# Q, K and V projections in two pairs of tiles, another pretended time for the first U gathers, and an output projection in plain f32

## The chip, the core and the metric

The kernel runs on one core of one Trainium2 chip. The metric is the device time of one execution in microseconds (us); the median of three runs is given. Five engines work side by side, each through its own instructions in a fixed order: TensorE (PE, with its weight loads as PEld), VectorE (DVE), ScalarE (ACT), GpSimd (POOL) and SyncE (SP). SP issues the plain DMAs, POOL the indirect ones (gathers).

## What is computed

512 tokens of 1024 features pass through two layers, all in float32. Layer 0 mixes tokens by sliding-window attention, layer 1 by a short gated convolution, and each is followed by PEER, a retrieval of experts:

```python
def peer_ffn(xn, w_query, sub_keys, expert_u, expert_v):
    q = (xt @ w_query).reshape(T, PEER_HEADS, 2, QUERY_HALF)
    s = jnp.einsum('thpd,hpnd->thpn', q, sub_keys)
    ...
    u = jnp.take(expert_u, ic, axis=0)
    a = jnp.einsum('td,thkd->thk', xc, u)
    w = gc * jax.nn.gelu(a, approximate=False)
    v = jnp.take(expert_v, ic, axis=0)
    return jnp.einsum('thk,thkd->td', w, v)

for i in range(DEPTH):
    h = rmsnorm(x, norm_mix[i])
    x = x + (attention(h) if i % 2 == 0 else short_gated_conv(h))
    h = rmsnorm(x, norm_ffn[i])
    x = x + peer_ffn(h, ...)
```

Each token picks 16 of 16384 experts for each of 8 heads, so 128 rows of `expert_u` and 128 of `expert_v`, of 4 KB each. The attention projects every token to 16 query heads, 4 key heads and 4 value heads (`w_qkv`), and its result with `w_o`.

## The kernel before

The tokens lie in four tiles of 128. PEER is done in two ways. For **tiles 2 and 3** it is dense (`dense`, L688): all 128 blocks of 128 experts are read and multiplied, and a table G of gates, zero for experts that are not picked, masks the result. One step of that loop is `ustep` (L700), three groups of eight `psA` matmuls, and `vstep` (L710), twelve `y` matmuls (L731). A float32 factor is split there into two float32r halves, high and low (`halves`, L693, one ACT cast and one DVE subtraction), and three products are summed. For **tiles 0 and 1** the picked rows are gathered (`gather`, L620): 128 U gathers (L631, 128 rows, one for each token, 512 KB), each followed by one DVE product and sum (L634), and then 128 V gathers (L662, the 128 rows of one token), of which PE takes two at a time (L672, four `acc` matmuls for a pair). Both kinds fill the same ring of six buffers (`gtile`, L612), two more in layer 1's front.

Four gathers run in the course of the kernel: layer 0 tile 0, layer 0 tile 1, layer 1 tile 0, layer 1 tile 1. They are called U0/V0, U1/V1, U2/V2 and U3/V3 here. The rest of the work is in four stages: the first front (attention, and routing of layer 0), the dense part of layer 0, the second front (convolution, routing of layer 1), and the dense part of layer 1.

The work is written as three Python generators (`stream_d` for fronts and dense parts, `stream_g` for the gathers, `stream_f` for what tiles 0 and 1 need besides), and `merge` (L810) decides in which order their pieces are written down. Each piece yields a number, the time that it is taken to last, and the stream that is furthest behind goes next. For one gather that number is `rate()` (L802): GR0 ahead of the front, the pair FR0 (U, V) in the first front, DR0 in the dense part. The order written is a priority: a scheduler then orders every engine's instructions when the kernel is built, and takes an earlier-written one first where both could go. The V matmuls get a head start (L668, HPF in the fronts and HPV in the dense parts). `stream_d` stops at `yield "g0_1"` (L921) until the gather of tile 1 in layer 0 is written: the convolution of tiles 1 to 3 begins with `xd[1]`, tile 1's result.

In the first front, `attn_qkv` (L229) projects tile 0 alone with pieces of `w_qkv` in the pool `wp` (`piece`, PE line L237); attention and routing of tile 0 follow (its first indices release U0); then it projects tiles 1, 2 and 3 with pieces in the attention's pool (`scpiece`). `attn` (L245) normalizes and rotates, makes scores, softmax and weighted values, and ends in `proj` (L181), the product with `w_o`. For tiles 1 to 3 that product is split (L189 to L200); for tile 0 it is plain f32 (L202).

Of the kernel before, what the change touches and what calls it, by code (L numbers as in the profile page):

```python
# [8 lines left out]
F32 = mybir.dt.float32  # L9
F32R = mybir.dt.float32r  # L10
# [5 lines left out]
ALU = mybir.AluOpType  # L16
# [3 lines left out]
P = 128  # L20
# [22 lines left out]
SCB = 4  # L43
# [5 lines left out]
GSC = 32768.0  # L49
GY = 1.7  # L50
FD0 = 100.0
QP = 3.0
GR0 = 1.3
DEC = 2
FD1 = 80.0
# [15 lines left out]
P3 = 1  # L71
# [3 lines left out]

DR0 = (2.4, 2.4)
DR1 = (2.5, 2.5)
FR0 = (3.0, 3.0)
FR1 = (3.0, 3.0)


# [1 line left out]
def trunk(ctx: ExitStack, tc: tile.TileContext, a: dict, out: bass.AP):  # L83
    nc = tc.nc
# [130 lines left out]
    def attn_norm(tiles, pool):  # L215
        gain = first.pop("gain", None) or gain_of(a["norm_mix"][0:1, :])
        res = []
        for t in tiles:
            if "x" in first:
                xs[t] = first.pop("x")  # L220
            else:
                xs[t] = b4.tile([P, D], F32, name="xq", tag="b4")
                nc.sync.dma_start(xs[t], a["x"][t * P:(t + 1) * P, :])
            hT = pool.tile([P, KC, P], F32, name="hTa", tag="hTa", bufs=4)
            normT(t, gain, hT, py)
            res.append(hT)
        return res
# [17 lines left out]
    def attn(tiles, qks, pool, L):  # L245
# [1 line left out]
        kT, vs, qkg, sink, nsink, cos, sin, mask = L  # L247
        nh = NH + NKV
        oTs = []
        sp = P3 and n > 1  # L250
        for j, t in enumerate(tiles):
            qk = qks[j]
            sq = pool.tile([P, nh, HD], F32, name="qsq", tag="qsq")
# [25 lines left out]
            for half in range(2):  # L279
# [3 lines left out]
                    nc.tensor.transpose(ps[:, k * P:(k + 1) * P],  # L283
                                        qk[:, 2 * hp:2 * hp + 2, :].rearrange("p a d -> p (a d)"), ident)
                nc.scalar.copy(qT[:, half * 4:half * 4 + 4, :], ps.rearrange("p (k t) -> p k t", k=4))
            if sp:
                oT = pool.tile([P, 2, 4, P], F32R, name="oTh", tag="hTa", bufs=4)
                oL = pool.tile([P, 2, 4, P], F32R, name="oTl", tag="qk", bufs=3)
            else:
                oT = oL = pool.tile([P, 2, 4, P], F32, name="oT", tag="hTa", bufs=4)  # L290
            oTs.append([(lambda k, o=o: o[:, k // 4, k % 4, :]) for o in (oT, oL)])
            if t == 0:
                k0, kw, moff, blks = 0, P, P, [0]
            else:
# [2 lines left out]
            for gp2 in range(2):  # L297
# [42 lines left out]
                    yield 6.0  # L340
                psov = pso.rearrange("p (r q) -> p r q", r=4)
                nc.scalar.copy(oT[:, gp2], psov)
                if sp:
                    nc.vector.tensor_tensor(oL[:, gp2], psov, oT[:, gp2], op=ALU.subtract)
        for t in tiles:
            xs[t] = pool.tile([P, D], F32, name="x", tag="x", bufs=3)
            nc.sync.dma_start(xs[t], a["x"][t * P:(t + 1) * P, :])
        yield from proj(a["wo"], oTs, tiles, py, (pool, ("sc", "sc"), SCB) if sp else None)

    def conv(tiles, pool, psum, slow=1.0):  # L350
        n = len(tiles)
# [506 lines left out]
    def stream_d():  # L858
        with tc.tile_pool(name="l0", bufs=1) as l0:
            def lc(name, shape, src=None):  # L860
                t = l0.tile(shape, F32, name=name)
                nc.sync.dma_start(t, a[name] if src is None else src)
                return t
            cos, sin = lc("cos", [P, NT, RH]), lc("sin", [P, NT, RH])
            mask = lc("mask", [P, 2 * P])
            qg1 = lc("qg1", [P, HD], bcast_row(a["q_norm"]))
            kg1 = lc("kg1", [P, HD], bcast_row(a["k_norm"]))
            sink = lc("sink", [P, NH], bcast_row(a["sinks"]))
            qkg = l0.tile([P, NH + NKV, HD], F32, name="qkg")
            nc.vector.tensor_copy(qkg[:, :NH, :], qg1.unsqueeze(1).to_broadcast([P, NH, HD]))  # L870
            nc.vector.tensor_copy(qkg[:, NH:, :], kg1.unsqueeze(1).to_broadcast([P, NKV, HD]))
            kT = l0.tile([P, NKV, S], F32, name="kT", tag="k8")
            vs = l0.tile([P, NT, NKV * HD], F32, name="vs")
            nsink = l0.tile([P, NH], F32, name="nsink")
            nc.vector.tensor_scalar(nsink, sink, -1.0, None, op0=ALU.mult)
            L = (kT, vs, qkg, sink, nsink, cos, sin, mask)
            flip = [0]

            def p2(name):
                flip[0] ^= 1  # L880
                return pmm(name) if flip[0] else pv.tile([P, 512], F32, name=name, tag="acc")

            def scpiece(src):
                w = l0.tile([P, KC, P], F32, name="wsc", tag="sc", bufs=SCB)
                nc.sync.dma_start(w, src)
                return w

            def run(g):
                for v in g:
                    if isinstance(v, list):  # L890
                        return v
                    yield v
            hTs = attn_norm([0], l0)
            yield 5.0
            qk0 = yield from run(attn_qkv([0], hTs, l0, L, py, piece, 1.75))
            hTs = attn_norm([1, 2, 3], l0)
            yield from attn([0], qk0, l0, L)
            r = st["p0_0"] = []
            yield from router(0, [0], None, py, None, r)
            st["r0_0"] = 1  # L900
            st["front"] = True
            st["pace"] = FS1
            qks = yield from run(attn_qkv([1, 2, 3], hTs, l0, L, p2, scpiece, QP))
            yield from attn([1, 2, 3], qks, l0, L)
            if GX0:
                st["gx"] = (l0, "sc", SCB)
            xnT = l0.tile([P, KC, 2 * P], F32, name="xnT", tag="k8")
            r = []
            yield from router(0, [1, 2, 3], l0, py, xnT, r)
# [78 lines left out]
```

## Time and profile before

| what | value |
|---|---|
| median of three runs | 3003.43 us (2999.48 to 3004.02) |
| the profiled execution | 2992.02 us, of which the span 2990.3 us |
| PE busy | 2626.9 us, 88% of the span |
| DVE busy | 2235.7 us, 75% |
| ACT busy | 1559.1 us, 52% |
| POOL busy | 1365.3 us, 46% |
| moved by DMA | 931.38 MB, mean 311 GB/s |

The span runs from the first to the last instruction of the program; the profiled execution's own time is 1.7 us longer. A share of 88% is a mean over stages: a stage in which PE is full sets its own length, one in which it is half empty has another limit. So the profile is read stage by stage below: with tables of busy time by stretch, where a count such as (x85) is the number of instructions in it; with the chain of waits that ended last; and with the instructions in order of time. In the trace an f32 matmul has two records.

### The profile page before, as it was taken

What the parts mean: (1) busy time and instruction counts of PE and PEld (TensorE: products, weight loads), DVE (VectorE), ACT (ScalarE), POOL (GpSimd) and SP (SyncE); (2) the same over time, 40 slices, a digit from 0 to 9 for tenths busy, and PEclk for the clock granted to TensorE, in tenths of its full rate; (3) what the DMA queues carried; (4) which work ended last, traced back from release to release, by engine and by line L of the source; (5) the groups of instructions that cost most, each with busy time, mean ns of one, the idle gap of its engine ahead of it and who ended that gap; (6) DMA issues with size and microseconds to landing.
All of it is one profiled execution on the core that took longest, in us unless ns stands there. A gap on an engine that the chain in (4) does not pass through costs nothing. (4 is left out here: it accounts for less than half of the span.)

```text
span 2990.3 us, 53463 instructions
## 1 busy us (share of the span) xinstructions
PE 2626.9 (88%) x19980; PEld 2083.9 (70%) x19980; DVE 2235.7 (75%) x5234; ACT 1559.1 (52%) x2384; POOL 1365.3 (46%) x1154
## 2 busy tenths in 40 slices
PE   5974699869999889999998689997888699999998
PEld 5762368636988767777787686773677577777897
DVE  2499849888998987446699774899899957446554
ACT  4224533685673458348444333358466449547543
POOL 0157733366344455534467424236566755554000
PEclk8986799989999999999999799997999899999999
DMA  5888988989999988998999867789999998998554
GB/s 199 283 315 306 341 293 276 329 308 382 365 353 389 323 318 290 345 328 291 363 408 396 310 220 279 249 319 318 363 349 360 345 359 297 333 317 302 192 189 157
DMA packets 263204, 931.38 MB, mean 311 GB/s; under 512 B 29984, under 2 KB 38560, under 8 KB 262944
## 3 DMA queue, kind: packets, MB, share of 16 engines
q0 software_dynamic: 147456, 536.94, 49.5%
q1 hardware_dynamic: 115488, 391.03, 36.3%
q8 instruction: 157, 2.57, 0.3%
q14 instruction: 103, 0.84, 0.1%
HBM read 916.31 MB, written 11.53 MB: 310 GB/s over the span
## 5 line engine op out<-in xcount | busy, mean ns | idle before, releaser
L631 POOL DMA_INDIRECT ug<-in_u_dram,idx x512 | 668.3, 1305 | 638.1 <-DVE act L634 312.5
L662 POOL DMA_INDIRECT vg<-in_v_dram,idxT x512 | 572.2, 1118 | 689.1 <-PE acc L672 571.7
L634 DVE CUSTOM_DVE_ANT_0 ug<-ug,xn 128x1024 f32<-128x1024 f32 x512 | 622.8, 1226 | 40.3 <-DMA ug<-in_u_dram,idx 39.3
L176 PE MATMUL psA<-xh,uh 128*128 128x256 f32 x2048 | 521.1, 292 | 46.0 <-ACT uh L696 19.0
L177 PE MATMUL psA<-xl,uh 128*128 128x256 f32 x2048 | 504.2, 284 | 0.0
L176 PEld LDWEIGHTS psA<-xh,uh 128*128 128x128 f32 x2048 | 391.1, 191 | 127.9 <-ACT wh L719 32.7
L697 DVE TENSOR_TENSOR ul<-du,uh 128x1024 fp32r<-128x1024 f32 x256 | 316.6, 1237 | 181.0 <-ACT uh L696 179.1
L697 DVE TENSOR_TENSOR vl<-dv,vh 128x1024 fp32r<-128x1024 f32 x256 | 316.2, 1235 | 145.2 <-ACT vh L696 121.8
L177 PEld LDWEIGHTS psA<-xl,uh 128*128 128x128 f32 x2048 | 392.0, 191 | 4.5 <-issue 0.5
L696 ACT CAST uh<-du 128x1024 fp32r<-128x1024 f32 x256 | 268.6, 1049 | 205.3 <-PE psA L177 172.6
L696 ACT CAST vh<-dv 128x1024 fp32r<-128x1024 f32 x256 | 268.5, 1050 | 162.7 <-PE y L731 139.7
L672 PE MATMUL acc<-vg,wd 128*32 128x512 f32 x2048 | 318.1, 635 | 31.4 <-DMA vg<-in_v_dram,idxT 30.9
L731 PE MATMUL y<-vh,wh 128*128 128x512 f32 x1024 | 290.2, 406 | 34.9 <-ACT vh L696 29.9
L179 PE MATMUL psA<-xh,ul 128*128 128x256 f32 x2048 | 288.7, 283 | 10.1 <-DVE ul L697 10.0
L731 PE MATMUL y<-vl,wh 128*128 128x512 f32 x1024 | 285.7, 401 | 12.8 <-DVE vl L697 12.8
L731 PE MATMUL y<-vh,wl 128*128 128x512 f32 x1024 | 285.5, 399 | 3.0 <-DVE wl L720 3.0
L179 PEld LDWEIGHTS psA<-xh,ul 128*128 128x128 f32 x2048 | 261.8, 189 | 21.8 <-DVE ul L697 16.6
L738 ACT COPY jr<-ijg 128x2048 f16<-128x2048 f16 x128 | 243.2, 1900 | 35.0 <-DVE oj L742 33.1
L731 PEld LDWEIGHTS y<-vh,wh 128*128 128x128 f32 x1024 | 179.4, 191 | 86.5 <-ACT vh L696 36.7
L731 PEld LDWEIGHTS y<-vl,wh 128*128 128x128 f32 x1024 | 190.1, 191 | 62.9 <-DVE vl L697 18.8
L731 PEld LDWEIGHTS y<-vh,wl 128*128 128x128 f32 x1024 | 194.8, 192 | 50.9 <-DVE wl L720 4.7
L742 DVE TENSOR_TENSOR oj<-jr,io 128x2048 f16<-128x2048 f16 x128 | 157.4, 1229 | 78.0 <-PE psG L751 66.7
(208 smaller groups left out, 4021.1 us busy)
## 6 DMA issues: line engine op xcount, KB each, us to landing
du<-in_uT_dram SPq DMA_DIRECT2D x256, 512.0 KB, 6.6
dv<-in_v_dram SPq DMA_DIRECT2D x256, 512.0 KB, 5.9
wpc<-in_wq_dram SPq DMA_DIRECT2D x64, 512.0 KB, 4.8
wpc<-in_w_in_dram SPq DMA_DIRECT2D x48, 512.0 KB, 5.9
wpo<-in_wo_dram SPq DMA_DIRECT2D x16, 512.0 KB, 7.5
ug<-in_u_dram,idx POOLq DMA_INDIRECT x512
vg<-in_v_dram,idxT POOLq DMA_INDIRECT x512
wpo<-in_w_out_dram SPq DMA_DIRECT2D x16, 512.0 KB, 5.2
```

The costliest lines, as they stand in the source:

```text
L176: nc.tensor.matmul(ps, w[0][:, k, :], x[0][:, k, ts], start=(k == 0), stop=False)
L177: nc.tensor.matmul(ps, w[0][:, k, :], x[1][:, k, ts], start=False, stop=False)
L179: nc.tensor.matmul(ps, w[1][:, k, :], x[0][:, k, ts], start=False, stop=(k == KC - 1))
L631: nc.gpsimd.indirect_dma_start(out=ug, out_offset=None, in_=a[f"u{l}"], in_offset=bass.IndirectOffsetOnAxis(ap=r["idx"][h][:, c:c + 1], ax ...
L634: nc.vector.tensor_tensor_reduce(out=ug, in0=ug, in1=xn, scale=1.0, scalar=0.0, op0=ALU.mult, op1=ALU.add, accum_out=act[:, s:s + 1])
L662: ld = nc.gpsimd.indirect_dma_start(out=vg, out_offset=None, in_=a[f"v{l}"], in_offset=bass.IndirectOffsetOnAxis(ap=idxT[:, tt:tt + 1], ax ...
L672: mm = nc.tensor.matmul(acc[c:c + 32, :], wd[:, j, r8, :], vgs[j][:, h * 512:(h + 1) * 512], start=(q == 0 and r8 == 0), stop=(q == 3 and ...
L696: nc.scalar.copy(hi, w)
L697: nc.vector.tensor_tensor(lo, w, hi, op=ALU.subtract)
L731: nc.tensor.matmul(ys[tt][h], x[:, tt * P:(tt + 1) * P], m[:, h * 512:(h + 1) * 512], start=first and k == 0, stop=last and k == len(terms ...
L738: nc.scalar.copy(jr, ijg[:, 0, t0:t0 + TG].unsqueeze(2).to_broadcast([P, TG, P]))
L742: nc.vector.tensor_tensor(oj, jr, io128.unsqueeze(1).to_broadcast([P, TG, P]), op=ALU.is_equal)
```

## The change

Four things are changed. `attn_qkv` is called for tiles 0 and 1 together, so each of the twelve weight pieces that it loads serves two tiles, and later for tiles 2 and 3; `attn` still runs for tile 0 first and then for 1, 2 and 3. The pretended time of the second projection's pieces goes from 3.0 to 2.0 (QP). The pretended time of a U gather in the first front goes from 3.0 to 6.0 (FR0). The output projection of tiles 1 to 3 is done in plain f32, without the halves `oTh`, `oTl`, `woh` and `wol`.

```diff
-QP = 3.0
+QP = 2.0
...
-FR0 = (3.0, 3.0)
+FR0 = (6.0, 3.0)
...
-        sp = P3 and n > 1
...
-            if sp:
-                oT = pool.tile([P, 2, 4, P], F32R, name="oTh", tag="hTa", bufs=4)
-                oL = pool.tile([P, 2, 4, P], F32R, name="oTl", tag="qk", bufs=3)
-            else:
-                oT = oL = pool.tile([P, 2, 4, P], F32, name="oT", tag="hTa", bufs=4)
-            oTs.append([(lambda k, o=o: o[:, k // 4, k % 4, :]) for o in (oT, oL)])
+            oT = pool.tile([P, 2, 4, P], F32, name="oT", tag="hTa", bufs=4)
+            oTs.append([lambda k, o=oT: o[:, k // 4, k % 4, :]])
...
-                if sp:
-                    nc.vector.tensor_tensor(oL[:, gp2], psov, oT[:, gp2], op=ALU.subtract)
...
-        yield from proj(a["wo"], oTs, tiles, py, (pool, ("sc", "sc"), SCB) if sp else None)
+        yield from proj(a["wo"], oTs, tiles, py, None)
...
-            hTs = attn_norm([0], l0)
+            hTs = attn_norm([0, 1], l0)
             yield 5.0
-            qk0 = yield from run(attn_qkv([0], hTs, l0, L, py, piece, 1.75))
-            hTs = attn_norm([1, 2, 3], l0)
-            yield from attn([0], qk0, l0, L)
+            qk01 = yield from run(attn_qkv([0, 1], hTs, l0, L, py, piece, 3.5))
+            hTs = attn_norm([2, 3], l0)
+            yield from attn([0], qk01[:1], l0, L)
...
-            qks = yield from run(attn_qkv([1, 2, 3], hTs, l0, L, p2, scpiece, QP))
-            yield from attn([1, 2, 3], qks, l0, L)
+            qks = yield from run(attn_qkv([2, 3], hTs, l0, L, p2, scpiece, QP))
+            yield from attn([1, 2, 3], qk01[1:] + qks, l0, L)
```

The changed file is seven lines shorter from L287 on, so a line number there is up to seven less (L672 is now L665).

PE at the start of the program, before (`hTa` are the normalized and transposed tokens, `psq` the projection, `psk` and `psqT` the start of tile 0's attention):

```order
L153 MATMUL psT<-ident,h 128x128 x8
L237 MATMUL psq<-wpc,hTa 128x128 x96
L153 MATMUL psT<-ident,h 128x128 x24
L276 MATMUL psk<-ident,kd 128x128 x4
L283 MATMUL psqT<-ident,qk 128x128 x8
```

and now:

```order
L153 MATMUL psT<-ident,h 128x128 x16
L237 MATMUL psq<-wpc,hTa 128x128 x192
L153 MATMUL psT<-ident,h 128x128 x16
L275 MATMUL psk<-ident,kd 128x128 x4
L282 MATMUL psqT<-ident,qk 128x128 x8
```

Tile 1's transposes and its 96 projection matmuls now stand ahead of tile 0's attention.

PE at the end of layer 0's dense part, before (`y` are the last sums of the dense part, `psT` the transposes with which the convolution of tiles 1 to 3 begins, tile 1 first, `psbcu` its matmuls):

```order
L731 MATMUL y_4419<-vl,wh 128x512
L731 MATMUL y_4420<-vl,wh 128x512
L375 MATMUL psT<-ident,h 128x128 x24
L176 MATMUL psbcu_17265<-hh,whi 128x384
L176 MATMUL psbcu_17303<-hh,whi 128x384
```

and now:

```order
L724 MATMUL y_4091<-vl,wh 128x512
L724 MATMUL y_4092<-vl,wh 128x512
L665 MATMUL acc<-vg,wd 32x512 x88
L368 MATMUL psT<-ident,h 128x128 x24
L176 MATMUL psbcu_17101<-hh,whi 128x384
```

88 `acc` matmuls, those of the last 22 pairs of V1, stand between the dense part and the convolution. Before, the last pair of V1 stood ahead of step 96 of the 128 dense steps; now the first 42 pairs stand ahead of step 88 and none between there and the end.

POOL at the same place, now (`vg` are V1's gathers and then V2's, `ug` U2's, `wd` the weights that a V gather's rows are multiplied with, `dw` products of dense steps):

```order
L655 DMA vg<-in_v_dram,idxT 128x1024 x4
L706 TENSOR_TENSOR dw<-dw,G 128x256 x13
L655 DMA vg<-in_v_dram,idxT 128x1024 x14
L647 MEMSET wd 128x512
L655 DMA vg<-in_v_dram,idxT 128x1024 x16
L655 DMA vg<-in_v_dram,idxT 128x1024 x8
L624 DMA ug<-in_u_dram,idx 128x1024 x8
L624 DMA ug<-in_u_dram,idx 128x1024 x120
L655 DMA vg<-in_v_dram,idxT 128x1024 x22
```

All 128 gathers of U2 stand behind the last of V1, in one piece with no dense product between them. In the order of before, 83 reductions of U2 stood on DVE ahead of the last `vl` of layer 0's dense part.

## Rows read from the trace of the kernel before

**Rows 1.** The page: gather queue (packets, MB, share of 16 engines), one plain load (us to landing).

```profile
q0 software_dynamic: 147456, 536.94, 49.5%
...
dv<-in_v_dram SPq DMA_DIRECT2D x256, 512.0 KB, 5.9
```

**Rows 2.** Busy time by stretch: length, PE, PEld, DVE, ACT, POOL, PEclk, DMA share, GB/s.

```profile
0.00:40.00 40.00, 27.81 (x208) 27.20 (x208) 4.30 (x11) 9.80 (x23) 1.19 (x6) 0.96 0.86 312
...
150.00:357.00 207.00, 117.09 (x683) 83.49 (x681) 201.22 (x586) 88.23 (x243) 137.88 (x116) 0.74 0.90 317
...
1453.00:1645.00 192.00, 172.65 (x1049) 147.97 (x1047) 185.91 (x284) 80.84 (x121) 128.17 (x93) 1.00 1.01 399
1645.00:1675.00 30.00, 6.24 (x26) 5.21 (x26) 27.89 (x51) 10.12 (x18) 20.47 (x17) 0.57 1.00 385
1675.00:1791.00 116.00, 104.99 (x578) 102.83 (x577) 83.53 (x138) 37.89 (x50) 33.99 (x29) 0.96 0.70 240
1791.00:1850.00 59.00, 53.13 (x262) 32.49 (x264) 22.11 (x30) 18.75 (x27) 24.82 (x22) 0.97 0.72 259
1850.00:1975.00 125.00, 123.58 (x956) 97.57 (x949) 103.34 (x542) 47.91 (x109) 42.07 (x44) 1.00 0.76 262
1975.00:2092.00 117.00, 92.14 (x1075) 58.74 (x1073) 109.61 (x434) 96.33 (x109) 64.49 (x59) 0.85 0.93 332
```

**Rows 3.** Stretches as before, instructions on the tile ug alone: DVE, POOL, PEclk, DMA, GB/s.

```profile
1453.00:1645.00 192.00, 103.11 (x85) 125.83 (x90) 1.00 1.01 399
1645.00:1675.00 30.00, 17.10 (x16) 15.85 (x13) 0.57 1.00 385
1675.00:1791.00 116.00, 35.23 (x29) 31.43 (x26) 0.96 0.70 240
```

**Rows 4.** Stretches as before, instructions on the tile acc alone: PE, PEld, ACT, the rest alike.

```profile
1453.00:1645.00 192.00, 2.99 (x24) 0.57 (x24) 2.31 (x4) 1.00 1.01 399
...
1791.00:1850.00 59.00, 15.20 (x92) 2.71 (x96) 0.00 (x0) 0.97 0.72 259
1850.00:1975.00 125.00, 29.66 (x160) 5.06 (x152) 0.00 (x0) 1.00 0.76 262
1975.00:2092.00 117.00, 37.10 (x224) 5.36 (x224) 2.31 (x4) 0.85 0.93 332
```

**Rows 5.** The ends of both dense parts, instructions on the tile y alone: PE, PEld, DVE.

```profile
1453.00:1645.00 192.00, 96.94 (x401) 72.65 (x399) 0.00 (x0) 1.00 1.01 399
...
2805.00:2978.00 173.00, 100.74 (x420) 76.82 (x420) 0.34 (x1) 1.00 0.54 176
```

**Rows 6.** Timeline of PE between two dense steps: start, us, engine, line, what, records.

```profile
1447.15 1.06 PE L672 MATMUL acc<-vg,wd 128*32 128x512 f32 x8
1448.14 0.39 PE L176 MATMUL psA<-xh,uh 128*128 128x256 f32 x1
```

**Rows 7.** Timelines of the first front: projection, output projection plain and split, DVE's splits.

```profile
23.13 16.16 PE L237 MATMUL psq<-wpc,hTa 128*128 128x128 f32 x128 [3.30 <-DMA wpc<-in_wqkv_dram]
...
43.43 1.47 DVE L259 TENSOR_TENSOR qk<-qk,qr 128x1280 f32<-128x1280 f32 x1
...
90.19 5.32 PE L202 MATMUL pswo<-wpo,oT 128*128 128x512 f32 x12
...
357.39 1.22 DVE L192 TENSOR_TENSOR wol<-wpo,woh 128x1024 fp32r<-128x1024 f32 x1
...
359.67 0.69 DVE L344 TENSOR_TENSOR oTl<-pso,oTh 128x512 fp32r<-128x512 f32 x1
...
362.00 0.39 PE L200 MATMUL pswo<-woh,oTl 128*128 128x512 f32 x1
362.23 0.40 PE L199 MATMUL pswo<-wol,oTh 128*128 128x512 f32 x1
```

**Rows 8.** Timeline at the start of the second front, ACT and POOL.

```profile
1655.26 1.06 ACT L143 ACTIVATE h<-x 128x1024 f32<-128x1024 f32 x1 [8.62 <-DMA x<-xd]
...
1656.30 0.94 POOL L631 DMA_INDIRECT ug<-in_u_dram,idx  x1 [0.31 <-issue]
```

## The prediction

> **What bounds the kernel now.** I read first the busy time by stretch. No engine sets the whole span. From 150 to 357 us, in the first front, DVE is busy 201 of 207 us and PE 117: the reductions of U0 and the attention of three tiles share DVE. In the last 192 us of layer 0's dense part PE is busy 173, DVE 186, and the DMA engines are full at 399 GB/s, since U2's gathers run beside the steps; no V work is left there but three pairs [rows 2 to 4]. Then comes a hole: for 30 us PE is busy 6.2, until tiles 1 to 3 are normalized and transposed; the convolution follows with PE busy 105 of 116 us, and the routing with 124 of 125 [rows 2]. The last stretch, 2805 to 2978 us, has no gather in it, and PE is never idle [rows 5].
>
> The gathers are a chain of their own, U0, V0, U1 to V3. It has slack at the end of the kernel (the last stretch runs without it), but one deadline: V1 must be done before the convolution begins. Before, it was done 32 steps early. What the profile must answer is what happens when that deadline is missed, since the new order of PE puts 22 of V1's 64 pairs between the last dense step and the convolution.
>
> **Why the pace does this.** FR0 relieves the first front of nothing: in the new order all 128 reductions of U0 still stand on DVE ahead of the routing of tiles 1 to 3, because DVE takes what is ready. But as a written order, every later gather moves back: at the end of layer 0's dense part by 127 places, 44 of V1 and 83 of U2. V1's tail is then written behind the dense steps, and PE, always ready with a step, takes it last. The ring holds six buffers, so POOL is three pairs ahead and then stands still.
>
> **The change, part by part.**
>
> *First front, +18 us.* 96 matmuls more (192 records) stand ahead of tile 0's attention; 128 records took 16.2 us, so 24 us [rows 7]. Some of this could lie in time that PE spends idle (12 of the first 40 us [rows 2]), but the order makes the first projection wait for tile 1's transposes too, so I count all. The twelve weight loads are the same number in all. From there DVE sets the pace, and it loses work: tile 1's three passes like that of 1.47 us and a dozen short ones (some 7 us) now lie earlier, six `oTl` of 0.69 us and three `wol` of 1.22 us are gone, two sums of some 0.7 us come in: 13 us less, and U0 ends 11 us later. The output projection costs PE more: 48 matmuls of two records, 0.44 us each, make 42.6 us; split, 144 at 0.23 us made 33.1 [rows 7]. Of these 9 us about a quarter lies under DVE's work, as 16 of the 48 stand ahead of the last reduction; 7 remain. Ends: +5, if half of the 24 us is hidden, to +30, if DVE's 13 us were not on the path.
>
> *Dense part of layer 0, -45 us.* The last stretch has no gathers and does 420 `y` matmuls in 173 us; at this rate the 401 of the stretch from 1453 us take 165 instead of 192 [rows 5]. That is 27 us, U2's reductions and three pairs included. The other 19 pairs leave the PE-bound steps ahead of it, at 0.99 us for a pair, from its start to the next matmul's [rows 6]: 19 us. Ends: -50 to -38.
>
> *The hole, +76 us.* After the last step three pairs are in the ring; the other 38 gathers come one by one. 1024 gathers took 49.5% of the 16 DMA engines' 2990 us [rows 1], 1.45 us for one with the engines to itself. 38 make 55 us. The last must land: a plain load of the same size takes 5.9 us from issue [rows 1]. Four copies of `acc` take 2.3 us [rows 4], the sum 1.2. Then tile 1's result is stored, loaded and normalized; that wait was 8.6 us [rows 8]. It is hidden, because the new order puts 28 U2 reductions on DVE between that sum and the third tile's last transposed half, all needing a gather: 28 at 1.45 are 41 us. In all 105 us from the last step to the convolution, where it was 30 with 16 reductions [rows 2, 3]. Ends: POOL issues one in 0.94 plus 0.31 us [rows 8], and DVE needs 1.22 for a reduction [rows 3], which makes 47 + 9 + 34 = 90, so +60; beside dense steps 90 gathers took 192 us, 2.13 each [rows 3], which makes 81 + 9 + 60, so +120. I take the value from the queue's own share, since little else is loaded in that hole.
>
> *Convolution, +12.* 58 reductions stand beside it on DVE instead of 27. 31 at 1.22 us are 38; DVE had 32 us idle [rows 2, 3]. So it is full, and its idle time, waits for PE within each chunk, cannot all be used. Ends +5 to +32.
>
> *Rest of the second front, 0.* 40 reductions come in: 19 up to 1850 us, where DVE is busy 22 of 59, and 21 in the routing, 26 us where 22 were idle. In return 19 of 30 pairs leave, from stretches where PE is full [rows 2, 4]. Ends -10 to +10.
>
> *Dense part of layer 1, +14.* These 19 pairs come back: 7 while the first gates are made (PE busy 92 of 117 us [rows 2], 28 pairs there now [rows 4]), for 2 us, and 12 in the first 16 steps at 1 us. U3 and V3 move back by eight steps, and the gather-free end shrinks from 32 steps to about 24, still enough to hide them. Ends +10 to +26.
>
> The sum is 18 - 45 + 76 + 12 + 0 + 14 = **+75 us** on an execution of 2992.0 us, hence 3067. The median of the runs is 11.4 us above that execution, so I add 75 to it: **3078**.
>
> **The rivals.**
>
> *Gathers at POOL's own pace.* Alone in the hole, the gathers might run as fast as POOL issues them, 1.25 us, with DVE just behind: the lower end above, +60 in place of +76, 3062. For it: POOL's rows show 0.94 us with 0.31 between [rows 8]. Against it: the queue's share of 1.45 us. The Trainium skill ("DMA: Bandwidth & Descriptors", section "Anatomy of one DMA — SWDGE (gpsimd) path") fits a gather-type DMA as 2.0 us plus its bytes at 436 GB/s; for 512 KB that is an estimate of 3.2 us alone and 1.2 us of transfer, by which the hole would be some 46 + 7 + 34 us and the sum +56. The fullest stretch here moved 399 GB/s [rows 2], so the trace doesn't reach that rate.
>
> *Gathers at the crowded pace.* If the convolution's weights (24 loads of 512 KB) and U2 hold each other up as dense loads did, the hole costs +120: 3122. For it: the DMA share is 1.00 in the hole already [rows 2]. Against: in the hole SP has few loads to issue, since its queue soon stands at the store of tile 1's result.
>
> *The first front pays for it (no change).* If the 96 matmuls fit into PE's idle time, DVE's 13 us come off in full, and the output projection, without its waits for `woh` and `wol`, with a third done early, ends 18 us sooner, then the front gives 31 us back. With the hole and the rest at their lower ends (-45 + 60 + 5 + 0 + 10) that is -1: 3002. It decides at the start: tile 0's attention must begin no later than before. Against it: 24 us of matmuls and 12 us of idle time.
>
> **How the numbers follow.** Forecast 0.55, POOL's pace 0.18, crowded pace 0.15, no change 0.06; 0.06 is for a gain that I don't see, as the first front's order has changed in many places. The range goes from 3030, which takes in POOL's pace with a cheaper front, to 3125, the crowded pace. 0.2%, 6 us, is about what a measurement of this kernel can tell from no change: faster by more 0.07, within 0.05, slower by more 0.88.
>
> **What would show it.** In the busy time by stretch: a hole of about 105 us after layer 0's last `y`, with PE under a third busy and a granted clock below the 0.57 of before; 44 V gathers and then U2 in it; in the dense part before it some 40 steps without any gather. Tile 0's first U gather some 24 us later; the stretch from the last reduction of U0 to the second transposes about 7 us longer. I am wrong if the hole is under 60 us, or if the first front is shorter than before.

## The result, and the profile after

The changed kernel takes 3078.84 us (median of 4 runs, 3073.1 to 3087.9), the kernel before 3001.47 beside it: a ratio of 1.026, with a 95% interval of 1.0233 to 1.0287. It is slower, by 77 us where +75 was forecast. Its profiled execution took 3078.74 us, with a span of 3076.9, and that of before 2990.3: 86.7 us more, which the stages account for as follows (each stage ends at the event named, in us of its own length).

| stage, up to | before | after | difference | forecast |
|---|---|---|---|---|
| first front: first `y` | 672.3 | 690.7 | +18.4 | +18 |
| dense part of layer 0: last `y` | 972.3 | 933.3 | -39.0 | -45 |
| the hole: first `psbcu` | 29.9 | 110.5 | +80.6 | +76 |
| convolution: last `yl` | 118.4 | 122.8 | +4.4 | +12 |
| rest of the second front: first `psA` | 172.4 | 150.7 | -21.7 | 0 |
| first gates and steps of layer 1: first `y` | 126.6 | 147.9 | +21.3 | +14 |
| dense part of layer 1: last `y` | 886.4 | 909.1 | +22.7 | (in the 14) |

Busy time by stretch, changed kernel (length, PE, PEld, DVE, ACT, POOL, PEclk, DMA share, GB/s), to be laid beside [rows 2]:

```profile
1360.00:1467.00 107.00, 105.74 (x1069) 92.50 (x1068) 78.16 (x89) 87.14 (x120) 22.97 (x20) 1.00 0.56 190
1467.00:1624.00 157.00, 157.00 (x966) 140.52 (x964) 85.87 (x110) 73.77 (x110) 0.00 (x0) 1.00 0.54 175
1624.00:1734.50 110.50, 42.05 (x201) 10.18 (x200) 45.78 (x77) 12.34 (x21) 77.45 (x75) 0.62 0.95 361
1734.50:1857.00 122.50, 116.33 (x621) 111.81 (x621) 120.79 (x205) 40.15 (x51) 82.53 (x63) 0.96 0.99 376
1857.00:1896.00 39.00, 27.84 (x121) 22.28 (x120) 36.56 (x59) 14.13 (x20) 23.16 (x18) 0.91 0.98 366
1896.00:2008.00 112.00, 106.64 (x832) 90.84 (x830) 108.12 (x517) 40.07 (x96) 47.92 (x43) 0.97 0.82 280
2008.00:2156.00 148.00, 110.45 (x1200) 67.25 (x1200) 132.49 (x518) 107.19 (x127) 79.61 (x74) 0.87 0.92 331
```

In the last 157 us of layer 0's dense part POOL does nothing at all, and the DMA engines move 175 GB/s where they moved 399 [rows 2]: the last gather before the hole was issued at 1370.9 us, and the last 45 steps or so run without one. Then PE works for 42 of 110 us. After it the roles in the second front are turned: DVE is full in the convolution (120.8 of 122.5 us, 83.5 of 116 before [rows 2]), and the gates of layer 1 have more `acc` work beside them. The reductions of U2 and the pairs of V2 by the same stretches, on the tiles ug (DVE, POOL) and acc (PE, PEld, ACT), show where the gathers went, to be laid beside [rows 3, 4]:

```profile
1624.00:1734.50 110.50, 33.31 (x28) 40.02 (x34) 0.62 0.95 361
1734.50:1857.00 122.50, 72.89 (x61) 82.53 (x63) 0.96 0.99 376
1857.00:1896.00 39.00, 22.34 (x19) 23.16 (x18) 0.91 0.98 366
1896.00:2008.00 112.00, 25.51 (x22) 18.50 (x14) 0.97 0.82 280
...
1624.00:1734.50 110.50, 36.34 (x176) 5.47 (x176) 2.30 (x4) 0.62 0.95 361
...
1896.00:2008.00 112.00, 16.29 (x88) 2.65 (x88) 0.00 (x0) 0.97 0.82 280
2008.00:2156.00 148.00, 47.77 (x288) 6.96 (x288) 2.30 (x4) 0.87 0.92 331
```

176 records of `acc` in the hole are 22 pairs (8 records each), as the prediction had read from the order; the 28, 61, 19 and 22 reductions are close to the 28, 58, 19 and 21 that it counted there (one that spans a border is counted on both sides). What the hole is made of stands in the timeline of PE in it (start, us, engine, line, what, and in brackets the wait ahead of it and what ended it):

```profile
1622.96 1.07 PE L724 MATMUL y<-vl,wh 128*128 128x512 f32 x4
1634.97 5.90 PE L665 MATMUL acc<-vg,wd 128*32 128x512 f32 x32 [10.94 <-issue]
1644.57 1.94 PE L665 MATMUL acc<-vg,wd 128*32 128x512 f32 x8 [3.70 <-DMA vg<-in_v_dram,idxT]
1647.12 1.94 PE L665 MATMUL acc<-vg,wd 128*32 128x512 f32 x8 [0.62 <-DMA vg<-in_v_dram,idxT]
...
1689.34 1.75 PE L665 MATMUL acc<-vg,wd 128*32 128x512 f32 x8 [0.62 <-DMA vg<-in_v_dram,idxT]
1717.15 1.97 PE L368 MATMUL psT<-ident,h 128*128 128x128 f32 x8 [26.06 <-DVE h L146]
...
1732.75 1.94 PE L368 MATMUL psT<-ident,h 128*128 128x128 f32 x8 [10.02 <-DVE h L146]
1734.51 1.01 PE L176 MATMUL psbcu<-hh,whi 128*128 128x384 f32 x2
```

It has three pieces. For 11 us PE waits although three pairs have been lying in the ring, the last of them issued at 1370.9 us. Then a pair comes every 2.56 us in most cases (2.63 in the mean), from 1644.57 to 1689.34. From 1691 on there is no V work; PE waits for DVE, which has the three norms (`h`) in one queue with 28 reductions. The first piece was in no term of the prediction, and POOL's timeline says what it is:

```profile
1624.79 0.97 POOL L655 DMA_INDIRECT vg<-in_v_dram,idxT  x1 [171.95 <-DVE cc L397]
1626.07 1.11 POOL L655 DMA_INDIRECT vg<-in_v_dram,idxT  x1 [0.30 <-issue]
1637.16 0.94 POOL L655 DMA_INDIRECT vg<-in_v_dram,idxT  x1 [9.98 <-PE acc L665]
1638.40 0.94 POOL L655 DMA_INDIRECT vg<-in_v_dram,idxT  x1 [0.30 <-issue]
```

POOL has stood for 172 us (it had nothing else to do since 1452 us) at one V gather, and what released it is not a matmul of `acc` but DVE's first instruction on a tile of the second front's pool (`cc`, L397), right behind the last dense step. That gather writes one of the two extra buffers, which lie in that pool (`GX1`, and `st["gx"]` set in `stream_d`), and the pool's memory is the dense part's until the last step. The order in which PE waits for the pairs shows which pair it is. The gathers take eight completion semaphores in turn, and the waits of five consecutive pairs in PE's program, the 42nd to the 46th of V1, are

```
L665 MATMUL acc<-vg,wd 32x512 [waits DMASW3_49,DMASW2_49]
L665 MATMUL acc<-vg,wd 32x512 [waits ...,DMASW3_49,...,DMASW2_49,...,PE_49,Pool_49]
L665 MATMUL acc<-vg,wd 32x512 [waits DMASW5_49,DMASW4_49]
L665 MATMUL acc<-vg,wd 32x512 [waits DMASW7_49,DMASW6_49]
L665 MATMUL acc<-vg,wd 32x512 [waits DMASW1_49,DMASW0_49]
```

(in the second, the dots are eight waits for loads: the memory of its buffers was the dense part's, into which these loads went). Had the 43rd pair been gathered in its turn, it would wait for 5 and 4. It waits for 3 and 2, which come round again behind the 46th: POOL ran ahead with pairs 44 to 46, these filled all six buffers, and PE, which adds up the pairs in order, could take none of them without the 43rd. So nothing of V1 could move until the dense part was over, whoever had time for it.

### The profile page after: what moved, and what is told of

Its sections match the earlier page's. It is cut to its first block, busy times and chain, and to the rows that moved or that the text cites. A ratio compares the mean times of both kernels' runs of the same rounds, so it can differ in the third digit from the quotient of the medians.

```text
span 3076.9 us, 53338 instructions
## 1 busy us (share of the span) xinstructions
PE 2651.2 (86%) x19932; PEld 2078.1 (68%) x19932; DVE 2223.4 (72%) x5211; ACT 1542.2 (50%) x2372; POOL 1342.5 (44%) x1163
## 5 line engine op out<-in xcount | busy, mean ns | idle before, releaser
L624 POOL DMA_INDIRECT ug<-in_u_dram,idx x512 | 653.3, 1276 | 638.4 <-DVE act L627 264.8
L655 POOL DMA_INDIRECT vg<-in_v_dram,idxT x512 | 556.4, 1087 | 783.7 <-PE acc L665 488.3
L665 PE MATMUL acc<-vg,wd 128*32 128x512 f32 x2048 | 327.1, 669 | 65.5 <-DMA vg<-in_v_dram,idxT 49.9
L731 ACT COPY jr<-ijg 128x2048 f16<-128x2048 f16 x128 | 244.5, 1910 | 42.7 <-DVE oj L735 41.6
```

The costliest lines, as they stand in the source:

```text
L624: nc.gpsimd.indirect_dma_start(out=ug, out_offset=None, in_=a[f"u{l}"], in_offset=bass.IndirectOffsetOnAxis(ap=r["idx"][h][:, c:c + 1], ax ...
L655: ld = nc.gpsimd.indirect_dma_start(out=vg, out_offset=None, in_=a[f"v{l}"], in_offset=bass.IndirectOffsetOnAxis(ap=idxT[:, tt:tt + 1], ax ...
L665: mm = nc.tensor.matmul(acc[c:c + 32, :], wd[:, j, r8, :], vgs[j][:, h * 512:(h + 1) * 512], start=(q == 0 and r8 == 0), stop=(q == 3 and ...
L731: nc.scalar.copy(jr, ijg[:, 0, t0:t0 + TG].unsqueeze(2).to_broadcast([P, TG, P]))
```

## The experiments

The experiments ran on three chips, on which the kernel before takes 3048.7 us (first to fourth), 3044.4 (fifth to eighth) and 3041.6 (ninth to twelfth): each time is compared with that of before on its own chip. In the stage tables the kernel of the fourth run (before, with the plain product) stands for the kernel before there, from which it differs by less than can be measured. A stage table shows one profiled execution of each kernel, up to 11 us off its median (the third's is 9 us above, the eighth's and the eleventh's are 11 above and below), and columns can be of different chips: a few us between two columns say nothing.

**The parts alone.** Four kernels take the change apart: the pairs of tiles with the plain product, but the old pace; the pace alone; the pairs alone (with pace and product as before, QP as changed); the plain product alone.

```diff
 first:  changed kernel    -FR0 = (6.0, 3.0)  +FR0 = (3.0, 3.0)
 second: kernel before     -FR0 = (3.0, 3.0)  +FR0 = (6.0, 3.0)
 third:  changed kernel, pace as in the first, oTh/oTl and the split proj of before put back
 fourth: kernel before     -sp = P3 and n > 1 +sp = False      (in attn)
```

> The changed kernel with the U gathers' pretended time in the first front back at 3.0. In the built order V1 is then done before the dense part of layer 0 ends, and 76 reductions of U2 stand ahead of its last step. Theory (the pace alone makes the hole and all that follows it): no hole; what is left is the first front's cost, 18 to 23 us, so 3020 to 3025 us. Rival (the order of projections and the plain product cost the time, the hole is paid back by the dense part): 3055 us or more. A hole would be 100 us or more from the last y to the first psbcu; without one it is about 30 us.

> The kernel before with only the pretended time of a U gather in the first front set from 3.0 to 6.0. In the built order 21 of V1's pairs stand between the last dense step and the convolution. Theory: the first front stays as it was (within 6 us), the dense part of layer 0 gains 39 to 45 us, the hole costs 76 to 81, convolution and the second dense part 18 to 30: 3055 to 3065 us. Rival: within 10 us of the kernel before.

> The projections in two pairs of tiles alone: pretended time 3.0, and the output projection split as before. Theory: tile 0's attention starts 22 to 24 us later, DVE is relieved of 7 us of tile 1's normalization, so the first front is 14 to 18 us longer and the run takes 3015 to 3020 us. Rival (PE has the idle time to take the 96 matmuls): first front within 5 us, 3000 to 3006 us. Beside the run with the plain product it says what that product is worth: by the prediction 0, at most 5 us either way.

> The kernel before with only the output projection of tiles 1 to 3 in plain f32. PE has 9 us more of matmuls there, DVE 8 us and ACT 8 us less. Theory: 0, within 6 us of the kernel before (2996 to 3007 us). Rival (the waits for the halves were on the path): 10 to 18 us faster, 2984 to 2992 us.

Measured: pairs and plain product 3096.0 us, a ratio of 1.0165 (1.0146 to 1.0184); the pace alone 3102.5, 1.0184 (1.0164 to 1.0204); the pairs alone 3087.7, 1.0131 (1.0114 to 1.0148); the plain product alone 3050.6, 1.0005 (0.9991 to 1.0018). The stages, in us:

| stage, up to | 4th: before, plain | 2nd: pace alone | 1st: pairs, plain | 3rd: pairs |
|---|---|---|---|---|
| first `y` | 680.0 | 680.6 | 699.5 | 715.3 |
| last `y` of layer 0 | 991.1 | 938.0 | 1010.8 | 1003.5 |
| first `psbcu` | 30.0 | 114.4 | 28.4 | 31.1 |
| last `yl` | 117.0 | 122.4 | 119.5 | 114.0 |
| `psA` of layer 1 | 175.6 | 152.6 | 173.7 | 178.3 |
| first `y` of layer 1 | 144.9 | 160.2 | 141.8 | 133.3 |
| last `y` | 901.0 | 918.6 | 902.1 | 907.3 |

The pace alone makes the hole, and leaves the first front as it is; the pairs alone make the first front longer, and no hole; the plain product alone costs nothing that can be measured. Beside the pairs it isn't settled: the medians of the first and the third are 8 us apart, with intervals that just touch, and their profiled executions lie the other way round (3089.8 and 3096.8). So the expectations held in their places (no hole without the pace, a first front that the pace leaves alone, a plain product at 0), and +54 for the pace lies where it was expected, though its dense part gained 53 us and not 39 to 45. The times of the first and the third did not hold: the pairs cost 39 to 47 us and not 14 to 23, of which 12 to 20 lie in the dense part of layer 0, where the code is the same and only the places of the gathers are known to differ. QP, for which the prediction has no term, is 2.0 in every kernel with pairs; what it does by itself was not tried. The waits of POOL in the second of these kernels (what waited for what, us in total, times, longest) hold the same single wait as the changed kernel; the first, third and fourth kernel, and the kernel before, which have no hole, have no such row:

```profile
POOL vg L662 <- DVE cc L404: 177.6, 1, 177.6
```

**Is it the extra buffers?** The fifth run is the changed kernel again, beside the others. The sixth is the changed kernel with one statement moved, the ninth the kernel before with the pace of 6.0 and the same statement moved:

```diff
         with tc.tile_pool(name="f1", bufs=1) as f1:
-            if GX1:
-                st["gx"] = (f1, "gx", GX1)
             finish(0, st["ys"], f1)
             yield "g0_1"
+            if GX1:
+                st["gx"] = (f1, "gx", GX1)
             yield from conv([1, 2, 3], f1, py)
```

> The changed kernel, nothing else, beside the kernel before on the same chip, to see whether its parts add up. Alone, the pace of 6.0 cost +54 us and the pairs of tiles with the plain product +47. If the two effects are independent, they add up to about +100 us, a ratio of 1.033. If they share a cost (both push V1 and U2 back in the same steps), the sum is smaller: +77 us, the 1.026 of the first measurement.

> The changed kernel, with one statement moved: the gathers may use the two extra buffers of the second front's pool only once V1 is done, no longer from the end of the dense part on. Pace 6.0 stays. Theory: V1's tail is not held back by TensorE, but by its place in a ring whose seventh and eighth buffer come into being only when the dense pool closes; POOL stands 172 us at the first of them, and all gathers stand behind it. Then V1 is done within the dense steps again, the hole shrinks from 110 to about 30 us, the dense part gets its 40 to 50 us back, and the time is that of the pairs of tiles without the pace: a ratio of about 1.016, some 30 us under the changed kernel (if that stands at 1.026). Rival, the one of the prediction: TensorE prefers the dense steps because V1's tail is written behind them. Then the hole stays, and at most its first 11 us go: a ratio of 1.022 or more.

> The kernel before, with the pretended time of 6.0 for the first U gathers (which alone cost it +54 us) and with the two extra buffers given to the gathers only once V1 is done. Theory (the ring): the pretended time costs nothing by itself, it only put 22 pairs of V1 behind the first gather that waits for the extra buffers; with these given later, all pairs stand among the dense steps again, and no hole over 35 us is left. V1 stands some 6 to 8 pairs further back in the dense part than before, U2 by 15 places, so 0 to +15 us, a ratio of 1.000 to 1.005. Rival: the later place of U2 and V1 is a price of its own. Then the hole goes, but the dense end and the second front keep half of the +54: a ratio of 1.009 or more.

Measured: the changed kernel 3113.9 us, 1.0226 (1.0197 to 1.0255); with the statement moved 3078.6, 1.0107 (1.0081 to 1.0133); the kernel before with pace 6.0 and the statement moved 3037.8, 0.9989 (0.9978 to 1.0000). The pace is 6.0 in the last two, and the hole is gone from both. Busy time by stretch of the sixth kernel, the last 32 dense steps and the hole:

```profile
1512.00:1713.00 201.00, 163.44 (x969) 138.79 (x967) 186.20 (x283) 73.98 (x110) 134.56 (x85) 1.00 0.97 363
1713.00:1740.50 27.50, 5.76 (x25) 4.70 (x24) 23.15 (x40) 9.94 (x17) 17.15 (x14) 0.56 0.99 387
```

And of the ninth:

```profile
1476.70:1661.60 184.90, 167.15 (x1010) 140.64 (x1008) 164.82 (x252) 75.65 (x114) 112.81 (x84) 1.00 1.00 383
1661.60:1693.80 32.20, 5.75 (x25) 4.74 (x25) 28.88 (x51) 10.16 (x17) 23.56 (x19) 0.61 0.97 374
```

Holes of 27.5 and 32.2 us, with PE busy under 6 of them, are the hole of before [rows 2]. So the pretended time costs nothing as a place in the order: what costs is that it moved V1's 43rd pair behind the statement that hands out the extra buffers. The prediction's own cause (PE prefers the dense steps, because V1's tail is written behind them) is refuted: in the sixth kernel the tail is written in the same place, and PE takes it among the dense steps. In the wait tables of both kernels the row of 172 us is gone too. The ninth kernel is the fastest of the study, 3.7 us under the kernel before, but its interval ends at 1.0000, and 6 us was what a measurement can tell.

The parts do not add up: +54 for the pace and +47 for the pairs are 101 us, the whole change on its chip +70. Without the hole, the pairs make the dense part of layer 0 longer (1004.9 us in the sixth kernel, 980.1 in the ninth, on another chip; 1010.8 and 991.1 in the first and the fourth, on one); with it, the last 45 steps have no gather, and the dense part takes 933.8 us with pairs and 938.0 without. The hole hides that part of their price.

**What the reductions in the hole cost.** In the seventh and eighth kernels (the changed one and the one before) U2's normalized tile is loaded only when the third tile of the convolution is normalized and transposed, so that no reduction of U2 can stand ahead of the convolution; the gather of U2 is also written only behind the convolution's norms:

```diff
+        if n > 1:
+            st["hl"] = hl
+            st["cn"] = 1
...
         xn = gp.tile([P, D], F32, name="xn", tag="xn", bufs=1)
+        if l == 1 and t == 0:
+            nc.vector.tensor_copy(xn[:, :1], st["hl"][:, KC - 1, 3 * P - 1:])
         nc.sync.dma_start(xn, xnd[t])
...
         yield "r1_0"
+        yield "cn"
```

> The changed kernel, where the normalized tile that U2's reductions read is loaded only after the last of the three tiles of the convolution has been normalized and transposed (its first column is written from that tile's low half before the load). So none of U2's 128 reductions can stand on DVE ahead of the convolution. Theory: in the hole of 110 us the 28 reductions between the sum of V1 and the last transposed half take 41 us, and what is left without them is the wait for the stored tile (8.6 us), the norm and the transposes, some 20 us: the hole shrinks to 85 to 92 us, of which the convolution gives some 5 to 10 back, as 74 reductions stand beside it instead of 58. In all -10 to -15 us. Rival: the store, the load and the norm of tile 1 take the 41 us by themselves, with the reductions in their shadow: the hole stays within 5 us, and the time rises by up to 10 us.

> The kernel before, with the same edit: all of V1 within the dense steps, none of U2 (before: 83 reductions). It takes the two loads of the dense end apart. Theory of the prediction: U2's gathers and reductions cost the last 48 dense steps some 27 us of their 180, so these take about 155 us; the hole stays at 30, without reductions rather 25; then the 101 reductions that come later cost the convolution 4 to 12 us and the stretch up to the second dense part, with 21 pairs fewer in it, about nothing, and these pairs some 20 us in the second dense part: in all -15 to +5 us. Rival: the dense end is slow by its own loads and eviction copies, not by U2; then it stays at 180, and the rest makes the kernel 20 to 30 us slower.

Measured: 3151.8 us, 1.0353 (1.0329 to 1.0376), 38 us above the changed kernel, and 3080.9, 1.0121 (1.0099 to 1.0144), 37 above the kernel before. The stages beside their partners:

| stage, up to | 5th: changed | 7th: U2 later | 4th: before, plain | 8th: before, U2 later |
|---|---|---|---|---|
| last `y` of layer 0 (from first `y`) | 933.8 | 937.0 | 991.1 | 963.8 |
| first `psbcu` | 117.5 | 99.5 | 30.0 | 21.2 |
| last `yl` | 125.8 | 146.2 | 117.0 | 146.0 |
| `psA` of layer 1 | 150.6 | 171.4 | 175.6 | 169.1 |
| first `y` of layer 1 | 151.9 | 167.3 | 144.9 | 167.2 |
| last `y` | 913.9 | 921.3 | 901.0 | 926.3 |

Both local expectations came true: the hole lost 18 us, and the dense part without U2 27 us, as the prediction priced it. The totals did not: U2's 128 reductions, now all behind the hole, were expected to find room in the second front, and did not. Busy time by stretch in the convolution, and the reductions in it, of the seventh kernel:

```profile
1736.10:1882.30 146.20, 123.89 (x628) 117.74 (x628) 137.73 (x233) 40.26 (x51) 100.58 (x74) 0.92 0.93 350
...
1736.10:1882.30 146.20, 88.61 (x75) 100.58 (x74) 0.92 0.93 350
```

The changed kernel has 62 reductions there in 125.9 us on that chip, and DVE full; 13 more make it 20 us longer. So going from some 30 reductions to some 61 cost the convolution 4 to 9 us in all, and each one beyond that 1.5; the same holds in the routing (36 in place of 22, and 22 us more).

**A further dose of the first term.** The tenth kernel is the sixth with the projections of three tiles first, and then one:

```diff
-            hTs = attn_norm([0, 1], l0)
-            qk01 = yield from run(attn_qkv([0, 1], hTs, l0, L, py, piece, 3.5))
-            hTs = attn_norm([2, 3], l0)
-            qks = yield from run(attn_qkv([2, 3], hTs, l0, L, p2, scpiece, QP))
+            hTs = attn_norm([0, 1, 2], l0)
+            qk01 = yield from run(attn_qkv([0, 1, 2], hTs, l0, L, py, piece, 5.25))
+            hTs = attn_norm([3], l0)
+            qks = yield from run(attn_qkv([3], hTs, l0, L, p2, scpiece, QP))
```

> The changed kernel with the two extra buffers given after V1 (1.011 of the kernel before on this chip) and with the projections of tiles 0, 1 and 2 first, then that of 3, in place of two and two: a further dose of the first term. Theory (a projection ahead of tile 0's attention is paid in full): the first U gather comes another 20 to 25 us later, at 172 to 176 us, and the first y of the dense part 15 to 28 us later than with two, at 723 to 736; the rest as it is; a ratio of 1.016 to 1.020. Rival (DVE sets the first front, and what PE does early it saves later): the first gather comes later, but the first y within 6 us of 708; a ratio of 1.011.

Measured: 3094.5 us, 1.0175 (1.0158 to 1.0192). The first U gather is issued at 181.2 us, 30 later than with two tiles (151.1 in the sixth kernel) and 54 later than with one (127.5 in the ninth); the first `y` comes at 724.2, 16 later than with two (708.2). Ratio and first `y` lie in the theory's ranges, the first one at its lower end, and the gathers come later than it said. So a projection ahead of tile 0's attention delays the gathers in full, but only a part of the delay, here about half, arrives at the dense part. The total rose from 1.0107 to 1.0175, 21 us.

**A try at a faster kernel.** The eleventh and twelfth are the kernel before with a quicker pretended pace of the gathers beside the first dense part, `DR0 = (2.0, 2.0)` and `(1.8, 1.8)` in place of `(2.4, 2.4)`.

> A try at a faster kernel: the kernel before, with a pretended time of 2.0 in place of 2.4 for the gathers beside the first dense part. It moves U2's gathers forward by some 12 places at the last dense step, and 17 pairs of V2 out of the second dense part into the second front. Putting U2 back by 83 places cost +38 us in all, less than half a microsecond for a place, 101 of them. Theory (gathers are the dearer the later they stand): -5 to -10 us. Rival (TensorE is full in the second front as in the second dense part, and a pair costs the same in both): within 5 us of the kernel before, or slower by up to 10, as the dense end has more gathers beside its full DMA engines.

> The same with 1.8: as many U2 gathers at the last dense step as with 2.0, but all 64 pairs of V2 done before the second dense part begins, 34 more than before. Theory (the later, the dearer): some -5 to -15 us; the second dense part starts later by some 30 us and is shorter by 35 or more. Rival (a pair costs the same in both): within 5 us of the kernel before.

Measured: 3089.4 us, 1.0166 (1.0148 to 1.0184), and 3099.1, 1.0186 (1.0169 to 1.0203). Both theories fell, and so did the rivals, which allowed 10 us and 5: the kernels are 48 and 58 us slower. V2 is done earlier, as planned, but U3 then comes into the stretch in which the first gates are made, and DVE is what sets that stretch already (121 of 145 us in the fourth kernel). Busy time in it and the reductions there, eleventh kernel:

```profile
2015.60:2212.80 197.20, 85.85 (x1014) 65.64 (x1014) 185.40 (x566) 106.00 (x120) 121.78 (x96) 0.68 0.89 309
...
2015.60:2212.80 197.20, 72.31 (x60) 84.50 (x64) 0.68 0.89 309
```

60 reductions take 72 us of DVE, and the stretch is 52 us longer than in the fourth kernel, with V2's pairs in it. It isn't the only loss: the dense part of layer 0 takes 1012.8 us (991.1 there), which was not followed up, and 43 us come back in the dense part of layer 1 (857.9 for 901.0). A V pair costs PE, a U reduction DVE: which of them may stand in a stretch depends on the engine that is free there, not on how early it is.

## Why the prediction was right, and where not

**First front, +18: measured +18.4.** The first U gather came 23.4 us later (24 predicted), the last reduction of U0 16.2 (11), the second transposes begin another 8.2 later (7); the routing and gates gave 6.0 back (0). So DVE's lost work returned 7 rather than 13 us, and what made up for it was not in the sum. The 7 us for the plain product are not its own: the fourth run, with that product alone, stands at +0.05% (-0.09 to +0.18). The stretch from the last reduction of U0 to the second transposes, which was to show them, takes 41.6 us there, as with the split product (42.2 in the kernel before, 41.9 in the second); with pairs of tiles it takes 49.8 (first kernel, plain) and 52.3 (third, split). Its ends in the fourth kernel, and then in the first:

```profile
364.38 1.23 DVE L634 CUSTOM_DVE_ANT_0 ug<-ug,xn 128x1024 f32<-128x1024 f32 x1 [1.66 <-DMA ug<-in_u_dram,idx]
407.22 3.38 PE L153 MATMUL psT<-ident,h 128*128 128x128 f32 x16
...
381.48 1.22 DVE L627 CUSTOM_DVE_ANT_0 ug<-ug,xn 128x1024 f32<-128x1024 f32 x1
432.51 3.68 PE L153 MATMUL psT<-ident,h 128*128 128x128 f32 x16 [3.48 <-DVE h L146]
```

Why the pairs make it longer stays open. So this term came out by luck: one part missed, one put down to the wrong cause, and a gain that it didn't have. On the chips of the experiments the same term was 20 to 28 us with the plain product. The rival in which the first front pays is out: tile 0's attention began later (at 73.2 us, 54.9 before), as its own condition said it must not.

**Dense part of layer 0, -45: measured -39.** By the two parts: 8 us more up to the 80th step, 47 less from there on. The steps without a gather ran as those of the last stretch do; for the `y` of both (PE, PEld, DVE, records as in [rows 5]):

```profile
1467.00:1624.00 157.00, 92.26 (x384) 70.39 (x384) 0.00 (x0) 1.00 0.54 175
...
2915.00:3065.00 150.00, 86.29 (x360) 66.03 (x360) 0.63 (x2) 1.00 0.52 173
```

0.409 and 0.417 us for one. The price of U2 beside the dense end, 27 us, was measured by the eighth run (963.8 us, 991.1 in the fourth, on another chip). The 8 us ahead of it were in no term.

**The hole, +76: measured +80.6.** The length was right, its reasons were not.
- *Why V1's tail is there.* The failing step is "PE, always ready with a step, takes it last". The order that the prediction read was right, its cause was the 43rd pair's place in an extra buffer; the sixth and ninth runs show it. The text ahead of the prediction names these two buffers, and the prediction counted only six.
- *The head.* That buffer's gathers can only be issued after the last step, and PE waits 10.9 us for them. No term held this.
- *The pace of V.* "38 gathers at 1.45 us" came from the queue's share of the DMA engines' time [rows 1]. In the hole a pair takes 2.56 us, 1.28 for a gather, and POOL issues one in 0.94 plus 0.30 us: that is POOL's own pace, the rival's price [rows 8]. The queue's share is 48.0% now, so that division would still give 1.44: it doesn't tell what a gather takes with the engines to itself. The page's row of the queue, and the time from issue to landing of both kinds of gather:

```profile
q0 software_dynamic: 147456, 536.94, 48.0%
...
ug<-in_u_dram,idx POOLq DMA_INDIRECT x512, 6.8
vg<-in_v_dram,idxT POOLq DMA_INDIRECT x512, 6.6
```

  The Trainium skill ("DMA: Bandwidth & Descriptors", section "Anatomy of one DMA — SWDGE (gpsimd) path") gives 1.2 us of transfer for such a gather and 3.2 us for one alone, by the estimate made ahead. The trace doesn't contradict the 1.2, but can't show it, since POOL issues one in 1.24 us; from issue to landing it has 6.6 to 6.8 us with others in flight, and no run here shows a gather alone.
- *The reductions.* 41 us from the end of V1's sum to the convolution was forecast, and 39.8 measured (1694.7 to 1734.5). But not as 28 gathers at 1.45: DVE was nearly full there. Busy time from the end of the sum on, and on the tile ug alone:

```profile
1694.70:1734.50 39.80, 5.68 (x24) 4.70 (x24) 36.92 (x65) 8.05 (x15) 32.18 (x26) 0.50 0.99 374
...
1694.70:1734.50 39.80, 30.85 (x26) 32.18 (x26) 0.50 0.99 374
```

  26 reductions make 30.9 us, the norms of three tiles 6, and 3 are idle. The seventh run took the reductions away: 18 us less, and what is left is the store and the load (a wait of 10.2 us at ACT) and the norms.

So too slow a pace (38 times 0.17 us, 6 us too much) stood against a head of 11 us that was missed. The hole of 110.5 us lies near the forecast of 105 because these nearly cancel. The mean granted clock in it was 0.62, not below 0.57 as the prediction would have seen it; PE was busy 42 of 110 us in it, and 6 of 30 before.

**Convolution, +12: measured +4.4.** The mis-sized term: DVE's 32 idle us could all be used, and it stood at 120.8 of 122.5. The seventh run shows how little was left behind it: 13 reductions more, and 20 us more.

**Rest of the second front 0 and dense part of layer 1 +14: measured -21.7 and +44.0.** Only their sum, +22 for +14, is near. The pairs that left this stage took more time with them than the reductions brought (150.7 us for 172.4), and they came back in the gates and the first steps: 288 records of `acc` beside the gates, where that stage, of 126.6 us, had 232 before (224 in the stretch of [rows 4]), and 21 us more, not 2. The prediction took PE's idle time there, 25 of 117 us [rows 2], as room; now 38 of 148 us are idle, so it was none. DVE is the busier engine in both, 110 and 132 us; that PE waits for it in turns is argued, not tried. The other 22.7 us, of which the forecast had 12, lie in the dense part with V2's and V3's pairs further back.

**The rivals.** POOL's pace was right in its price of a gather and wrong in its total, because the head and the reductions stood behind other waits. The crowded pace did not come: the hole moved 361 GB/s with nothing else of weight in it.

**The sum.** +75 was forecast and +77 measured, but the two causes aren't +18 and +57. Alone, the pace cost 54 us and the pairs with the plain product 47, and together 70: with the hole, the pairs no longer make the dense part longer (933.8 us with them, 938.0 without). The prediction had too little for the pairs and nothing for this overlap; that the two offset each other is luck.

## What to carry to other kernels

When work is late, ask first whether it could have been earlier: follow the one instruction at which its queue stands, and what releases that. A wait that ends with an instruction of another stage (here a copy in the next stage's pool) points to memory that is not there yet, and one buffer of that kind stops a ring that is in order on both sides, whatever the priorities say. Before gathers are moved between stages, list for each stage which engine has idle time, and put there only the kind of gather work that this engine does not do.

## What the runs showed of the hardware that was not expected

- An indirect gather of 512 KB lands 6.6 to 6.8 us after issue, and yet gathers follow one another at 1.28 us: POOL's 0.94 us of issue plus 0.30 between them sets the pace while few other transfers run, 364 GB/s over the 56 us of V1's tail.
- The same 85 or so U2 gathers beside the same 32 dense steps took 181 us at 399 GB/s in the fourth kernel and 201 us at 363 GB/s in the sixth; PE was busy 160 and 163 us. It isn't the chip: the first kernel, on that of the fourth, took 198 us at 359 GB/s. The kernels with two pairs of tiles and no hole had the longer dense part (1003 to 1011 us for 980 to 991), but it doesn't take pairs: the eleventh, without them, had 1012.8. Why the transfers get on worse there was not found; nothing was tried on it.
- The three chips of the experiments ran the kernel before in 3042 to 3049 us, 1.3 to 1.6% above the 3001.5 beside the result, at about the same mean granted clock (0.940 to 0.947 there, 0.947 in the profiled execution of before); the fourth kernel's dense parts and gates are the longer stages (991.1 us for 972.3, 144.9 for 126.6, 901.0 for 886.4).
